# A state space layer inside a decoder step: the recurrence over chunks in two halves of four groups

## The chip, the cores and the metric

The kernel runs on one core of one Trainium2 chip. The core has five engines with queues of their own: TensorE (PE; its weight loads are shown as PEld), VectorE (DVE), ScalarE (ACT), GpSimd (POOL) and SyncE (SP). Each works through its own instructions strictly in the order of the program; semaphores make an instruction wait for those of other engines. The metric is the device time of one execution, in microseconds; lower is better. Before the change it is 1601.29 us, the median of three runs (1599.1 to 1602.14).

## The reference, cut to what matters

The program is one layer of a decoder on a prompt of 1024 tokens and on 8 single sample tokens. One input projection feeds two branches, stick-breaking attention and a state space layer; both are gated, projected, merged and normalised. The change touches the state space layer: 64 groups of 16 channels, each with a complex state of 64 numbers that decays and turns from token to token.

```python
bu_re = jnp.einsum("gpc,bsgc->bsgp", bb_re, ug)
bu_im = jnp.einsum("gpc,bsgc->bsgp", bb_im, ug)
...
_, _, xr, xi = lax.associative_scan(_complex_affine_combine,
                                    (a_re_t, a_im_t, bu_re, bu_im), axis=1)
y = (jnp.einsum("gcp,bsgp->bsgc", c_re.astype(f), xr)
     - jnp.einsum("gcp,bsgp->bsgc", c_im.astype(f), xi)).reshape(bsz, s, D_SSM)
y = y + d_skip.astype(f) * uf
g = jax.nn.gelu(y)
```

## The kernel before, in words

**Stages.** The program first modulates the activations, then runs the attention of the prompt beside the input projection (to about 740 us), then the state space layer (about 743 to 1115 us), then the gated linear unit, the output projections, the merge and the normalisation. In all stages a stream of projection matmuls (line 144, tiles named pj) fills PE between the other steps: `Stream.weave` takes a list of steps and runs a share of the stream ahead of each, so the order on PE is written out by hand. A step has a cost and may have a due time, in the stream's own clock of 146 ns for a matmul; the stream runs on until the clock has reached the due time or its work is used up. The order on the other engines is chosen at build time by a scheduler with a model of costs; `high_priority(HURRY)` lets instructions go ahead of those traced up to 400 places earlier.

**The state space layer.** It goes by slabs f = 0 to 7 of 128 channels, that is 8 groups, or 4 pairs of groups. The prompt is cut into 128 chunks of 8 tokens. Within a chunk everything is a product; from chunk to chunk runs the recurrence. A slab has these steps (`SSM.steps`):

- `outputs(f - 1, b)` for b = 0, 1: the output products of the slab before, four groups each, two matmuls a group. One reads the slab's inputs (line 1052), the other the states xs at the chunks' starts (line 1053). Then a GELU on ACT and DVE (lines 1085 to 1090, tiles gh and gq) and a store. The due time is "xs", set 17000 ns of stream clock after the last input product.
- `inputs(f, e, b)`: the input products (line 1002). e is the group's place in its pair (partitions 0 to 63 or 64 to 127 of the state), b says which two of the four pairs. Each step is two matmuls, evacuated by ACT into sr and si, the real and imaginary part (lines 1004 and 1005), 128 chunk columns and 8 sample columns for every pair. The order is (e, b) = (0, 0), (0, 1), (1, 0), (1, 1).
- after (1, 1) `recur(f)`: the sample columns are copied aside by POOL (lines 1018, 1019); DVE turns sr and si by the phase tables ec and es (lines 1024 to 1029, six operations on 128x512), scans each pair's real and imaginary row with the decay r8 (line 1033, eight scans of 128 columns), and turns back into xs (lines 1038 to 1042, four operations on 128x512 and four on 64x512). POOL clears the first column of xs (line 1035) and copies the last states aside (line 1043).
- `tables(f + 1)`, `grouped(f + 1)` and `matrices(f + 1, b)`: loads and small products for the next slab (lines 926, 941, 947 and 956 among them).

**What runs between.** `SampleAttention` scores the sample tokens against the paged cache: POOL issues gathers into tile s_t (line 810), ACT copies two query columns (lines 823, 824), DVE multiplies and adds (line 833, s_sc), later the values (line 828, s_t). `tick` spreads its 122 pieces of work over the steps, two ticks to a step. So that the pieces keep pace with the layer, each first reads one column of `k.last`, a tile that the steps set: u when a slab's inputs are taken, sr after an input product with e = 1, gin in `matrices`, gh in the GELU. The first instruction of a gather (line 808, POOL), of a query copy (line 823, ACT) and of a value (line 818, DVE) is this read.

The projection's results are evacuated by ACT (line 1525 and 1527 for gates, line 975 for the layer's inputs) out of three PSUM tiles, and the weights' low parts are formed by POOL (line 109).

The tiles sr, si and xs have one buffer each, gh and gq two, and PSUM tile "a", which all products of the layer use, five.

Of the kernel before, what the change touches and what calls it, by code (L numbers as in the profile page):

```python
# [23 lines left out]
NCH = 128  # L24
# [125 lines left out]
class Stream:  # L150
# [63 lines left out]
    def weave(self, steps, until=0.0):  # L214

        n = len(steps)
        for i, (cost, ready, fn) in enumerate(steps):
            self.run(max(0.0, self.left - until) / (n - i + 1))
            want = ready() if ready else 0.0
            while self.clock < want and self.left > until + 1:  # L220
                if self.one() is False:
                    break
            fn()
            self.clock += cost
        self.drain(until)
# [248 lines left out]
def ssm_products(k, sp, io, f, b, after):  # L474
# [60 lines left out]
    for part_ in (phasors, inputs, outputs):  # L535
        part_()
        yield
# [3 lines left out]
class Attention:  # L541
# [189 lines left out]
    def steps(self, pairs):  # L731

        units = [(p, h, ms) for p in pairs for h in range(2) for ms in ((3, 0), (2, 1))]
        out = {p: [] for p in pairs}
        for u, (p, h, ms) in enumerate(units):
            s = self.score_steps(units[u + 1]) if u + 1 < len(units) else []
            t = [(860, (lambda key=(p, h, m): self.ready_at[key]) if j == ORDER[m][0] else None,
                  lambda t=(p, h, m, j): self.turn_step(t)) for m in ms for j in ORDER[m]]
            if not s:
                t += [(430, None, lambda: self.turn_step(None))] * LAG  # L740
            seq = []
            for n in (2, 2, 1, 1):
                seq += s[:n] + t[:1]
                s, t = s[n:], t[1:]
            out[p] += seq + t
        return self.score_steps(units[0]), out
# [154 lines left out]
class SSM:  # L901
# [91 lines left out]
    def inputs(self, f, e, b):  # L993
        k, nc, v = self.k, self.k.nc, self.v[f]
        if (e, b) == (0, 0):
            v["s"] = [self.t([128, 4, NCH + NS], n) for n in ("sr", "si")]
        sr, si = v["s"]
        half = slice(64 * e, 64 * e + 64)
        sp_ = self.ps.tile([128, 2, NCH + NS], F32, tag="a", name="sps")
        for i in range(2):  # L1000
            g = 2 * (2 * b + i) + e
            nc.tensor.matmul(sp_[:, i], v["gin"][:, g], v["ug"][:, g], start=True, stop=True)
        with k.tc.high_priority(HURRY):
            nc.scalar.copy(sr[half, 2 * b:2 * b + 2], sp_[0:64])
            nc.scalar.copy(si[half, 2 * b:2 * b + 2], sp_[64:128])
        if e == 1:
            k.last = sr[:, 2 * b, 0:1]
        if (e, b) == (1, 1):
            with k.tc.high_priority(HURRY):
                self.recur(f)  # L1010

    def recur(self, f):

        v = self.v[f]
        DVE, POOL = self.k.nc.vector, self.k.nc.gpsimd
        pr = slice(4 * f, 4 * f + 4)
        sr, si = v["s"]
        POOL.tensor_copy(self.ss[0][:, pr], sr[:, :, NCH:])
        POOL.tensor_copy(self.ss[1][:, pr], si[:, :, NCH:])
        ec, es = v["ec"], v["es"]  # L1020
        Z = [128, 4, NCH]
        t1, t2 = (self.t(Z, n, 2) for n in ("gh", "gq"))
        xr, xi = sr[:, :, 0:NCH], si[:, :, 0:NCH]
        DVE.tensor_tensor(t1, xi, es, ALU.mult)
        DVE.tensor_tensor(t2, xr, es, ALU.mult)
        DVE.tensor_tensor(xr, xr, ec, ALU.mult)
        DVE.tensor_tensor(xi, xi, ec, ALU.mult)
        DVE.tensor_tensor(xr, xr, t1, ALU.add)
        DVE.tensor_tensor(xi, xi, t2, ALU.subtract)
        for q in range(4):  # L1030
            r8 = v["r8"][:, q, 0:1].broadcast_to((128, NCH))
            for x in (xr, xi):
                DVE.tensor_tensor_scan(x[:, q], r8, x[:, q], 0.0, ALU.mult, ALU.add)  # L1033
        v["xs"] = xs = self.t([128, 4, 2, NCH + 1], "xs")
        POOL.memset(xs[:, :, :, 0:1], 0.0)
        for r in range(2):
            rows = slice(64 * r, 64 * r + 64)
            DVE.tensor_tensor(t1, xr, es if r else ec, ALU.mult)
            DVE.tensor_tensor(t2, xi, ec if r else es, ALU.mult)
            for e in range(2):  # L1040
                half = slice(64 * e, 64 * e + 64)
                DVE.tensor_tensor(xs[rows, :, e, 1:], t1[half], t2[half], ALU.add if r else ALU.subtract)
        POOL.tensor_copy(self.xf[:, 8 * f:8 * f + 8], xs[:, :, :, NCH].rearrange("p q e -> p (q e)"))
        self.mark("xs", 17000.0)

    def outputs(self, f, b):
        k, nc, v = self.k, self.k.nc, self.v[f]
# [16 lines left out]
    def steps(self, f):  # L1064

        R = lambda n: (lambda: self.at.get(n, 0.0))
        k = self.k
        two = lambda cost, n, fn, f: [(cost, R(n) if b == 0 and n else None, lambda b=b: fn(f, b)) for b in range(2)]
        out = []
        if f > 0:  # L1070
            out += two(1750, "xs", self.outputs, f - 1)
        if f < KT:
            out += [(454, R("ug") if (e, b) == (0, 0) else None, lambda e=e, b=b: self.inputs(f, e, b))
                    for e in range(2) for b in range(2)]
        if f + 1 < KT:
            out += [(0, None, lambda: self.tables(f + 1)), (0, lambda: k.taken.get(f + 1, 0.0), lambda: self.grouped(f + 1))]
            out += two(1300, "tab", self.matrices, f + 1)
        return out
# [14 lines left out]
    def finish_steps(self, last):  # L1093

        k, nc, io, out = self.k, self.k.nc, self.io, self.out
        PE, ACT, DVE, SP = nc.tensor, nc.scalar, nc.vector, nc.sync
        Z = [128, NPAIR, NS]
        v = {}

        def state():  # L1100
            h0 = [self.t(Z, n) for n in ("sr", "si")]
            SP.dma_start(h0[0], io["h0_re"])
            SP.dma_start(h0[1], io["h0_im"])
            v["cb"] = [self.t([128, NPAIR, 2, GC], n, 2) for n in ("gst", "tt")]
            for c, src in zip(v["cb"], ("c_re", "c_im")):
                nc.gpsimd.memset(c, 0.0)
                for e in range(2):
                    half = slice(64 * e, 64 * e + 64)
                    SP.dma_start(c[half, :, e], io[src][half])
            v["mask"] = self.t([128, 16, 32], "es", 2)  # L1110
            SP.dma_start(v["mask"], io["mask"])
            v["pick"] = self.t([128, NS], "r8", 2)
            SP.dma_start(v["pick"], io["pick"])
            v["dc"] = self.t([128, KT], "r8", 2)
            SP.dma_start(v["dc"], io["d_col"])
            ar, ai = (self.a1[:, :, n:n + 1].broadcast_to(Z) for n in range(2))
            t = self.t(Z, "hst")
            for dst, (a, x, op1), (b, y, op2) in (
                    (self.ss[0], (ar, h0[0], ALU.add), (ai, h0[1], ALU.subtract)),
                    (self.ss[1], (ar, h0[1], ALU.add), (ai, h0[0], ALU.add))):  # L1120
                DVE.tensor_tensor(t, a, x, ALU.mult)
                DVE.tensor_tensor(dst, dst, t, op1)
                DVE.tensor_tensor(t, b, y, ALU.mult)
                DVE.tensor_tensor(dst, dst, t, op2)
            v["ni"] = self.t(Z, "yy", 2)
            DVE.tensor_scalar(v["ni"], self.ss[1], -1.0, None, op0=ALU.mult)
# [598 lines left out]
```

## Time and profile before

The profiled execution took 1602.6 us; its span, from the first to the last instruction, is 1600.9 us.

| | whole span | 743 to 1115 us |
|---|---|---|
| length | 1600.9 us | 372 us |
| PE busy | 1490.8 us | 340.7 us |
| DVE busy | 1200.7 us | 300.6 us |
| ACT busy | 752.6 us | 149.1 us |
| POOL busy | 931.9 us | 215.7 us |
| granted PE clock | 0.969 | 0.96 |

How to read the lines that follow. A line of a timeline gives the start, the duration, the engine, the line of the code, the operation, the tiles written and read with their shape, how many such instructions follow one another, and, in brackets, how long the engine stood idle before it and what ended the wait. A line of waits gives the engine and line that waited, what for, the total, how often, and the longest. A line of a source view gives the shortest, median and longest duration in ns and the first and the last start. The granted clock is the share of full speed that the throttle gave PE. Busy times of PE include pipelining, so a busy PE is not PE at its peak.

### The profile page before, as it was taken

The numbers are of one execution on the slowest core, as the hardware profiler recorded it, in microseconds if no ns is written. First come the engines' busy times: TensorE is split into PE (matmuls) and PEld (weight loads), VectorE is DVE, ScalarE is ACT, GpSimd is POOL, SyncE is SP. The second block draws the span as 40 slices with busy tenths as digits, with TensorE's granted clock in tenths as the row PEclk, the third lists the DMA queues.
The fourth block names the chain that finished last, engine by engine and source line by source line (L and its number), as shares of the span: only waits on it lengthen the run. The fifth ranks groups of instructions, "written<-read, shape, count | busy, mean of one in ns | idle before, by whom it ended". The sixth has DMA issues, their size and how long they took to land.

```text
span 1600.9 us, 25589 instructions
## 1 busy us (share of the span) xinstructions
PE 1490.8 (93%) x9321; PEld 1412.0 (88%) x9321; DVE 1200.7 (75%) x1533; ACT 752.6 (47%) x1488; POOL 931.9 (58%) x800
## 2 busy tenths in 40 slices
PE   8889999999999999999999998899989968999997
PEld 4689999999999999999899998898789967999885
DVE  5558888888888889751899877788479986844566
ACT  3557777777777767654444443332442212311200
POOL 1738787878786878766565555554168761122064
PEclk9899999999999999999999998899989979999999
DMA  9333433433343434348779987867455678963322
GB/s 353 114 86 88 106 101 99 101 98 97 99 102 92 113 88 118 94 121 285 243 252 291 290 273 236 273 217 203 134 184 186 212 254 285 364 207 132 119 80 92
DMA packets 176731, 275.47 MB, mean 172 GB/s; under 512 B 46395, under 2 KB 119867, under 8 KB 176477
## 3 DMA queue, kind: packets, MB, share of 16 engines
q1 hardware_dynamic: 150555, 180.40, 36.5%
q0 software_dynamic: 23456, 84.95, 16.6%
q10 hardware_dynamic: 2594, 8.49, 2.0%
q8 instruction: 73, 1.20, 0.3%
q14 instruction: 53, 0.43, 0.1%
HBM read 196.77 MB, written 66.24 MB: 164 GB/s over the span
## 4 chain that ended last, share of the span: by engine, by line
PE 47%; DVE 24%; issue 8%; DMA 8%; POOL 6%; ACT 2%; SPq 1%; DVEq 0%; POOLq 0%; ACTq 0%
PE pj L144 29%; PE f L1402 6%; PE o L703 3%; PE z L657 3%; DVE s_sc L833 3%; DVE ke L668 3%; PE tp L686 3%; DMA l_t<-in_cache_v,l_idx 2%; DVE vs L639 2%; DVE be L669 2%; POOL s_t L810 2%; DVE l_t L889 1%; POOL wlo L109 1%; DVE sr L1033 1%; DVE s_t L828 1%
## 5 line engine op out<-in xcount | busy, mean ns | idle before, releaser
L144 PE MATMUL pj<-ahi,whi 128*128 128x344 f32 x2112 | 690.6, 330 | 20.1 <-ACT ahi L237 11.3
L144 PE MATMUL pj<-alo,whi 128*128 128x344 f32 x2112 | 684.2, 327 | 10.7 <-DVE alo L238 6.9
L144 PE MATMUL pj<-ahi,wlo 128*128 128x344 f32 x2112 | 478.5, 328 | 6.2 <-POOL wlo L109 6.2
L144 PEld LDWEIGHTS pj<-ahi,whi 128*128 128x128 f32 x2112 | 404.5, 192 | 27.6 <-ACT ahi L237 12.1
L144 PEld LDWEIGHTS pj<-alo,whi 128*128 128x128 f32 x2112 | 405.2, 192 | 15.2 <-DVE alo L238 8.3
L144 PEld LDWEIGHTS pj<-ahi,wlo 128*128 128x128 f32 x2112 | 362.9, 192 | 8.0 <-POOL wlo L109 6.8
L668 DVE TENSOR_TENSOR_SCAN ke<-ke,eye 128x896 f32<-128x896 f32 (+7 forms) x128 | 218.8, 1710 | 93.8 <-ACT ke L658 93.7
L109 POOL TENSOR_TENSOR wlo<-w,whi 128x1024 fp32r<-128x1024 f32 x53 | 133.6, 2520 | 204.8 <-PE pj L144 108.9
L658 ACT ACTIVATE ke<-z,nhb 128x448 f32<-128x448 f32 (+2 forms) x192 | 111.8, 582 | 81.3 <-PE z L657 79.3
L108 ACT CAST whi<-w 128x1024 fp32r<-128x1024 f32 x90 | 94.7, 1052 | 115.7 <-PE pj L144 73.1
L669 DVE TENSOR_TENSOR be<-be,ke 128x896 f32<-128x896 f32 (+7 forms) x128 | 125.0, 977 | 13.0 <-DVE ke L668 0.5
L833 DVE SCALAR_TENSOR_TENSOR s_sc<-s_t,s_q,s_sc 128x512 f32<-128x512 f32 x126 | 114.0, 905 | 27.3 <-DMA s_t<-in_cache_k,s_idx 15.8
L659 ACT ACTIVATE be<-z,hb 128x448 f32<-128x448 f32 (+2 forms) x192 | 110.6, 576 | 0.0
L686 PE MATMUL tp<-ident,be 128*128 128x128 f32 x576 | 88.9, 272 | 0.0
L810 POOL DMA_INDIRECT s_t<-in_cache_k,s_idx x64 | 69.6, 1088 | 30.1 <-issue 15.4
L495 POOL TENSOR_TENSOR pr<-tab 128x256 f32<-128x256 f32 x32 | 26.0, 813 | 90.6 <-DMA tab<-d_tab 80.3
L496 POOL TENSOR_TENSOR pt<-tab 128x256 f32<-128x256 f32 x64 | 75.9, 1187 | 3.1
L109 DVE TENSOR_TENSOR wlo<-w,whi 128x1024 fp32r<-128x1024 f32 x37 | 62.0, 1676 | 15.9 <-ACT whi L108 15.9
L689 ACT CAST wthi<-tp 128x512 fp32r<-128x512 f32 x96 | 56.7, 590 | 32.3 <-PE tp L686 29.9
L657 PE MATMUL z<-kl,qs 128*128 128x448 f32 (+2 forms) x192 | 65.9, 343 | 4.0 <-DMA kl<-kl 4.0
L690 DVE TENSOR_TENSOR wtlo<-tp,wthi 128x512 fp32r<-128x512 f32 x96 | 65.3, 680 | 5.6 <-ACT wthi L689 5.4
L657 PE MATMUL z<-kh,qs 128*128 128x448 f32 (+2 forms) x192 | 66.3, 345 | 0.9
(314 smaller groups left out, 2760.8 us busy)
## 6 DMA issues: line engine op xcount, KB each, us to landing
w<-in_w_in SPq DMA_DIRECT2D x38, 512.0 KB
w<-in_w_in POOLq DMA_DIRECT2D x26, 512.0 KB, 6.3
wc<-in_w_cond SPq DMA_DIRECT2D x24, 512.0 KB
d_a<-ox SPq DMA_DIRECT2D x128, 64.0 KB
gst<-d_gg SPq DMA_DIRECT2D x8, 576.0 KB
x<-in_xr SPq DMA_DIRECT2D x9, 512.0 KB
xt<-in_xt SPq DMA_DIRECT2D x8, 516.0 KB
d_sg<-gate SPq DMA_DIRECT2D x8, 516.0 KB
```

Of the source, the lines that this page charges most:

```text
L108: nc.scalar.copy(whi, w32)
L109: self.eng.tensor_tensor(wlo, w32, whi.bitcast(F32), ALU.subtract)
L144: PE.matmul(ps[c], w[:, blk(t)], x[:, cs(c)], start=(t == 0 and i == 0), stop=(t == KT - 1 and i == 2))
L657: nc.tensor.matmul(z[:, 0:wide], st["q", h][:, blk(i)], x[:, s:s + wide], start=j == 0, stop=j == 1)
L658: nc.scalar.activation(ke[:, s:s + cw], z[:, 0:cw], AF.Sigmoid, bias=k.nhb[:, hd:hd + 1], scale=-0.125)
L659: nc.scalar.activation(be[:, s:s + cw], z[:, 0:cw], AF.Sigmoid, bias=k.hb[:, hd:hd + 1], scale=0.125)
L668: nc.vector.tensor_tensor_scan(rev, rev, self.eye[:, NP - n:][:, ::-1], 0.0, ALU.mult, ALU.add)
L669: nc.vector.tensor_tensor(be, be, ke[:, 1:n + 1], ALU.mult)
L686: PE.transpose(tp[:, 2 * order[a] + e], w[e][:, blk(2 * j + a)], k.ident)
L810: nc.gpsimd.indirect_dma_start(out=tile[:, j].rearrange("p d s -> p (d s)"), out_offset=None, in_=self.io["cache_" + what], in_offset=bass ...
L833: DVE.scalar_tensor_tensor(sc, t, q[:, d - d0:d - d0 + 1], sc, op0=ALU.mult, op1=ALU.add)
L1402: PE.matmul(pp[c], a[:, token(i)], w[:, blk(c, 512)], start=(t == 0 and a is ah and w is wh), stop=(t == KT - 1 and a is al))
```

## The change

The recurrence of a slab is cut into two halves of two pairs (four groups) each. `recur(f, b)` does for the pairs 2b and 2b + 1 what `recur(f)` did for all four; it is called after each input product with e = 1, and the order of the input products becomes (e, b) = (0, 0), (1, 0), (0, 1), (1, 1), so that half 0's two products come first. The tile xs is taken at the first input product, the temporaries gh and gq are taken once for both halves, the due time "xs" is set by the second half as before. Tiles, buffers and PE's instructions are otherwise the same.

```diff
     def inputs(self, f, e, b):
         k, nc, v = self.k, self.k.nc, self.v[f]
         if (e, b) == (0, 0):
+            v["xs"] = self.t([128, 4, 2, NCH + 1], "xs")
             v["s"] = [self.t([128, 4, NCH + NS], n) for n in ("sr", "si")]
...
         if e == 1:
             k.last = sr[:, 2 * b, 0:1]
-        if (e, b) == (1, 1):
             with k.tc.high_priority(HURRY):
-                self.recur(f)
-
-    def recur(self, f):
+                self.recur(f, b)
+
+    def recur(self, f, b):
 
         v = self.v[f]
         DVE, POOL = self.k.nc.vector, self.k.nc.gpsimd
-        pr = slice(4 * f, 4 * f + 4)
-        sr, si = v["s"]
+        two = slice(2 * b, 2 * b + 2)
+        pr = slice(4 * f + 2 * b, 4 * f + 2 * b + 2)
+        sr, si = (x[:, two] for x in v["s"])
         POOL.tensor_copy(self.ss[0][:, pr], sr[:, :, NCH:])
         POOL.tensor_copy(self.ss[1][:, pr], si[:, :, NCH:])
-        ec, es = v["ec"], v["es"]
-        Z = [128, 4, NCH]
-        t1, t2 = (self.t(Z, n, 2) for n in ("gh", "gq"))
+        ec, es = v["ec"][:, two], v["es"][:, two]
+        if b == 0:
+            v["t"] = [self.t([128, 4, NCH], n, 2) for n in ("gh", "gq")]
+        t1, t2 = (t[:, two] for t in v["t"])
...
-        for q in range(4):
-            r8 = v["r8"][:, q, 0:1].broadcast_to((128, NCH))
+        for q in range(2):
+            r8 = v["r8"][:, 2 * b + q, 0:1].broadcast_to((128, NCH))
             for x in (xr, xi):
                 DVE.tensor_tensor_scan(x[:, q], r8, x[:, q], 0.0, ALU.mult, ALU.add)
-        v["xs"] = xs = self.t([128, 4, 2, NCH + 1], "xs")
-        POOL.memset(xs[:, :, :, 0:1], 0.0)
+        if b == 0:
+            POOL.memset(v["xs"][:, :, :, 0:1], 0.0)
+        xs = v["xs"][:, two]
...
-        POOL.tensor_copy(self.xf[:, 8 * f:8 * f + 8], xs[:, :, :, NCH].rearrange("p q e -> p (q e)"))
-        self.mark("xs", 17000.0)
+        POOL.tensor_copy(self.xf[:, 8 * f + 4 * b:8 * f + 4 * b + 4], xs[:, :, :, NCH].rearrange("p q e -> p (q e)"))
+        if b == 1:
+            self.mark("xs", 17000.0)
...
             out += [(454, R("ug") if (e, b) == (0, 0) else None, lambda e=e, b=b: self.inputs(f, e, b))
-                    for e in range(2) for b in range(2)]
+                    for b in range(2) for e in range(2)]
```

## The prediction, made before the changed kernel was run

> **What bounds the kernel now.** I read the page first, then busy time by stretch, then who TensorE waits for, then the order of instructions around those waits. The changed lines run in one stretch only, from the first input product (743 us) to the last output product (about 1115 us).
>
> ```profile
> span 1600.9 us, 25589 instructions
> ...
> 743.00:1115.00 372.00, 340.73 (x2201) 331.13 (x2200) 300.57 (x490) 149.09 (x385) 215.70 (x227) 0.96 0.82 262
> 790.00:835.00 45.00, 42.49 (x286) 41.12 (x285) 40.89 (x48) 17.14 (x51) 27.94 (x29) 1.00 0.82 266
> 835.00:880.00 45.00, 43.48 (x292) 42.18 (x292) 42.60 (x58) 21.31 (x64) 27.92 (x32) 1.00 0.92 289
> ```
>
> The columns are the stretch, its length, the busy time of PE, PEld, DVE, ACT and POOL with their instructions, the granted clock, the DMA share and GB/s. PE has 341 of the 372 us filled; it is the bound, and it stands for some 31 us. DVE has 301 us, but 40.9 and 42.6 of 45 in the second and third slab. The waits of PE in this stretch, and each one in the order of time:
>
> ```profile
> PE yp L1053 <- DVE xs L1042: 25.4, 9, 4.4
> PE pj L144 <- ACT gate L1525: 4.6, 1, 4.6
> PE pj L144 <- ACT zgate L1527: 1.2, 1, 1.2
> 776.71 0.49 PE L1053 MATMUL yp<-xs,gst 128*128 128x128 f32 x2 [3.94 <-DVE xs L1042]
> 868.05 0.49 PE L1053 MATMUL yp<-xs,gst 128*128 128x128 f32 x2 [1.51 <-DVE xs L1042]
> 913.70 0.49 PE L1053 MATMUL yp<-xs,gst 128*128 128x128 f32 x2 [2.52 <-DVE xs L1042]
> 962.67 0.79 PE L1053 MATMUL yp<-xs,gst 128*128 128x128 f32 x2 [4.21 <-DVE xs L1042]
> 1018.53 0.80 PE L1053 MATMUL yp<-xs,gst 128*128 128x128 f32 x2 [4.43 <-DVE xs L1042]
> 1021.66 0.80 PE L1053 MATMUL yp<-xs,gst 128*128 128x128 f32 x2 [1.91 <-DVE xs L1042]
> 1113.33 0.80 PE L1053 MATMUL yp<-xs,gst 128*128 128x128 f32 x2 [3.94 <-DVE xs L1042]
> ```
>
> In every slab PE arrives at the first half of the output products (b = 0) before the recurrence has written xs: 25.4 us in nine waits. These products also come out slow (0.63 to 0.80 us where 0.49 is usual), so I looked at the granted clock (after the instruction count) in the 8 us behind a wait:
>
> ```profile
> 868.00:876.00 8.00, 7.94 (x57) 1.00 0.72 275
> 776.00:784.00 8.00, 7.28 (x40) 0.79 0.91 304
> 913.00:921.00 8.00, 7.29 (x39) 0.79 0.58 208
> 962.00:970.00 8.00, 7.33 (x43) 0.79 0.54 195
> 1018.00:1026.00 8.00, 5.56 (x22) 0.50 0.97 359
> 1113.00:1121.00 8.00, 7.67 (x39) 0.60 0.28 98
> ```
>
> After the 1.51 us wait the clock stays at 1.00; after each wait of 2.5 us or more it falls. (1 - clock) x 8 us summed over the five low windows is 3 x 1.7 + 4.0 + 3.2 = 12.2 us. PE stood for 0.3 to 2.4 us inside them, so I take 10 us as a second price of the same waits. Together **35 us** hang on xs being late.
>
> [...]
>
> **The change part by part.** Why xs is late is seen in the fourth slab (f = 3):
>
> ```profile
> 881.83 0.62 PE L1002 MATMUL sps<-ug,gin 128*128 128x136 f32 x4
> 889.69 0.63 PE L1002 MATMUL sps<-ug,gin 128*128 128x136 f32 x4
> 889.13 8.57 DVE L833 SCALAR_TENSOR_TENSOR s_sc<-s_t,s_q,s_sc 128x512 f32<-128x512 f32 x8 [5.17 <-DMA s_t<-in_cache_k,s_idx]
> 897.62 0.69 DVE L1025 TENSOR_TENSOR gq<-sr,es 128x512 f32<-128x512 f32 x1
> 901.24 3.97 DVE L1033 TENSOR_TENSOR_SCAN sr<-r,sr 128x128 f32<-128x128 f32 x4
> 912.96 1.41 DVE L1042 TENSOR_TENSOR xs<-gh,gq 64x512 f32<-64x512 f32 x2
> ```
>
> The second input product is issued at 881.83, the fourth at 889.69. DVE stands 5.17 us for a gathered tile, scores eight columns of it, and only then begins the recurrence (897.62), which ends at 914.4.
>
> *Inputs reordered.* b outside e: the same four products in the same four steps. The first two now complete half 0, so it may begin two steps (7.9 us here) before the old one. PE gains or loses no instruction.
>
> *Half 0 ahead of half 1.* Output products b = 0 read pairs 0 and 1 only, and waits go by region: PE started at 913.70, when the first of the two xs writes of 912.96 was done (0.70 each) and the second was not. So b = 0 will wait for half 0 alone. Even if half 0 starts no sooner than the old recurrence and simply takes the first half of its time, it is early enough. Slab 3: the old one runs 897.6 to 914.4, its middle is 906, PE needs it at 913.7 - 2.5 = 911.2. The tightest is slab 5:
>
> ```profile
> 1000.03 0.68 DVE L1025 TENSOR_TENSOR gq<-sr,es 128x512 f32<-128x512 f32 x1
> 1017.79 3.81 DVE L1042 TENSOR_TENSOR xs<-gh,gq 64x512 f32<-64x512 f32 x2
> 873.44 0.38 PE L1052 MATMUL yp<-ug,tt 128*128 128x128 f32 x2
> ```
>
> It runs 1000.0 to 1021.6, middle 1010.8, needed at 1018.5 - 4.4 = 1014.1. The waits for b = 0 go: 25.4 us, with the 10 us of clock.
>
> *What is late next:* half 1 for b = 1, which PE reaches 5.4 us after b = 0 (868.05 to 873.44). In slab 3 that is 911.2 + 5.4 = 916.6; the whole recurrence, starting no sooner and 2.3 us longer (next point), ends at 916.7, just in time. In slab 5 it is needed at 1019.5 and ends at 1023.9, 4.4 us late. Bounds: nothing, if half 0 starts its two steps sooner, and 4.4 us in all eight slabs, 35 us. Most slabs are nearer to slab 3 (their waits above are shorter than slab 5's), so I take 3 us.
>
> *DVE, twice as many instructions.* 14 tensor operations per slab on 512 columns become 28 on 256; the eight scans stay.
>
> ```profile
> L1025 DVE TENSOR_TENSOR gq<-sr,es x8: 683/685/693, 754.7 to 1094.2; 128x512 f32<-128x512 f32 x8
> L1122 DVE TENSOR_TENSOR ssr<-ssr,hst 128x256 f32<-128x256 f32 x1 | 0.4, 426 | 0.1
> L1018 POOL COPY ssr<-sr x8: 214/363/734, 755.1 to 1091.8; 128x32 f32<-128x32 f32 x8
> L1043 POOL COPY xf<-xs x8: 181/327/1503, 777.4 to 1114.1; 128x8 f32<-128x8 f32 x8
> ```
>
> 2 x 426 - 685 = 167 ns per pair, 14 pairs: 2.3 us per slab, 19 us in all. DVE is idle 372 - 301 = 71 us of the stretch, so it hides there; with that cover gone it is the second rival.
>
> *POOL* gets three more copies per slab (two of the first kind and one of the second, 2 x 0.36 + 0.33 = 1.05 us, 8 us in all) beside 156 idle us. But two of its copies now wait in the middle of the recurrence, and behind them on its queue stand the issue of the gathers and the low parts of the weights (L109).
>
> *The pacing tile k.last.* From the second step on the sample's loads and query copies read sr[:, 0] after half 0's scan; until now they read it from the third step on, before the scan. So ACT (s_q copies), POOL (tile marks) and later DVE (s_acc) get a wait on half 0. Behind the ACT copies stand the evacuations of the third and fourth input product and of the projection's PSUM (L1525).
>
> ```profile
> ACT s_q L823 <- DVE sr L1033: 38.0, 5, 11.5
> 953.95 0.47 ACT L823 COPY s_q<-sr 128x1 f32<-128x1 f32 x4 [11.46 <-DVE sr L1033]
> 992.74 1.15 ACT L840 ACTIVATE s_ke<-s_sc,s_bias 128x1024 f32<-128x1024 f32 x1 [11.74 <-DMA w<-in_w_in]
> 995.21 0.66 PE L144 MATMUL pj<-ahi,whi 128*128 128x344 f32 x1 [4.63 <-ACT gate L1525]
> ```
>
> ACT already waits so once in five slabs. An ACT wait of 11.46 us cost PE nothing; one of 11.74 us cost it 4.63 us. The new waits are two per slab, each on half the work. Bounds: 0 (all below 11 us) and 4.6 us in each of eight slabs, 37 us. All five old ones together left PE at most its 1.2 us wait for zgate, so I stay near that end: 4 us.
>
> *After the stretch.* PE gets ahead of the sample's gathers, which DVE waits for as it is:
>
> ```profile
> DVE s_sc L833 <- DMA s_t<-in_cache_k,s_idx: 15.8, 4, 6.1
> DVE s_t L828 <- DMA s_t<-in_cache_v,s_idx: 9.6, 3, 6.1
> ```
>
> If these seven waits grow by what PE gains, part of it comes back at the end of the stretch, where layer outputs stand behind the scoring on DVE. Bounds 0 and the whole 25.4 + 10; I take 6 us, a quarter of the 25 us that DVE waits for gathers now.
>
> **Sum**: 25.4 + 10 - 3 - 4 - 6 = 22 us off. The profiled execution took 1602.6 us (span 1600.9 and 1.7 around it), 1.3 us above the median of 1601.29. 1602.6 - 22 = 1580.6, by the median **1579 us**.
>
> **Rivals.** (1) *Forecast*, 12 to 36 us off: 1565 to 1589.
>
> (2) *DVE or the gathers hold PE.* For: 42.6 of 45 us in slab 2, a DMA share of 0.82 to 0.92, and the order on DVE, which is fixed and puts scores that wait for a gather ahead of the recurrence (889.13). Against: DVE's 301 + 19 = 320 us is less than PE's 341. Then half 1 is late in all eight slabs by 2.2 us, half way between slab 3 and slab 5: 18 us of the 35 are lost, and 6 to 10 more behind the stretch. That leaves 7 to 11 off, about 1592 us.
>
> [...]
>
> (3) *ACT is held* (the slower side). The s_q copies stand ahead of the evacuations of products three and four, and half 0 is late because DVE stands at a gather. It decides from an ACT wait of about 11.5 us. The price is 4.63 us and 1.7 us of clock (as above) per slab, 51 us in eight, less the 35: 16 slower, 1617; from six slabs on (38 us) the kernel is slower. Against: half 0 has only 6 x 0.43 us on DVE ahead of its scans, and the five ACT waits of now cost next to nothing.
>
> (4) *No effect within 3 us*: the order on DVE leaves half 0 behind the same scores and new waits eat the rest, 1598 to 1604. That waits go by whole tiles, so that half 0 would wait for all four evacuations, is excluded by 913.70.
>
> **How the numbers follow.** Forecast 0.55, rival 2 0.18, rival 4 0.10, rival 3 0.17. Faster by over 0.2% (3 us, about what a measurement of this kernel can tell): 0.55 + 0.18 = 0.73; within 0.10; slower 0.17. The range runs from the forecast's best end, 1565, over rivals 2 and 4 to 1605, which leaves rival 3 and a little more out.
>
> **What would show it.** Right: PE's wait for xs falls from 25.4 to under 6 us; the first DVE operation of half 0 comes before the fourth input product; the clock over the stretch rises from 0.96 to about 0.99; DVE busy there is up some 19 us; the stretch is 20 to 30 us shorter. Wrong: PE waits at L144 for L1525 in several slabs (3); b = 1 products wait for xs while b = 0 do not, or DVE never idles (2); the stretch is shorter but waits for gathers or for L1224 and L1225 behind it have grown as much (the last term).

## The result and the profile after

The changed kernel takes 1589.78 us (median of 6 runs, 1585.67 to 1591.82), the kernel before, timed beside it, 1599.62 us (1595.86 to 1602.14). The ratio is 0.9932, interval 0.9914 to 0.9949: faster by some 10 us, where 22 were forecast. The profiled spans differ by 10.8 us (1600.9 and 1590.1). First, where the span lost it. These are the source views of the line of the input products and of the line of the output products' first matmuls, of before and of after (shortest, median and longest duration in ns, first and last start):

```profile
L1002 PE MATMUL sps<-ug,gin x128: 277/279/280, 743.8 to 1090.9; 128*128 128x136 f32 x128
L1052 PE MATMUL yp<-ug,tt x128: 270/275/422, 772.4 to 1120.2; 128*128 128x128 f32 x128
```

```profile
L1003 PE MATMUL sps<-ug,gin x128: 277/279/280, 742.8 to 1074.4; 128*128 128x136 f32 x128
L1056 PE MATMUL yp<-ug,tt x128: 270/275/421, 771.4 to 1104.1; 128*128 128x128 f32 x128
```

The stretch from the first start of the one to the last start of the other went from 376.4 to 361.3 us, 15.1 shorter. Ahead of it 1.0 us is gained, which the change can't reach; what follows it went from 480.7 to 486.0, 5.3 longer. So -1.0 - 15.1 + 5.3 = -10.8.

What PE waits for in this stretch and just behind it, in the changed kernel (total, times, longest):

```profile
PE pj L144 <- ACT gate L1529: 12.7, 6, 5.1
PE pj L144 <- ACT zgate L1531: 5.7, 1, 5.7
PE ycr L1158 <- DVE yy L1130: 4.4, 1, 4.4
...
PE pj L144 <- ACT u L975: 1.5, 1, 1.5
PE pj L144 <- ACT us_s L977: 1.4, 1, 1.4
PE yp L1057 <- DVE xs L1045: 1.0, 1, 1.0
```

The nine waits for xs, 25.4 us, have become one of 1.0. But PE's waits for ACT at the projection, 4.6 + 1.2 = 5.8 us before, are 12.7 + 5.7 + 1.5 + 1.4 = 21.3. So 24.4 us went and 15.5 came; and ycr, the first product behind the stretch, waits 4.4 us where it waited 1.4. The clock, first the one low window of before that the prediction did not count, then those of after (the clock stands behind the last instruction count):

```profile
995.00:1003.00 8.00, 7.79 (x36) 7.79 (x37) 7.86 (x15) 4.16 (x8) 4.38 (x4) 0.69 0.54 153
```

```profile
820.00:828.00 8.00, 7.07 (x33) 7.07 (x34) 5.23 (x6) 5.37 (x15) 7.67 (x6) 0.59 0.89 336
942.00:950.00 8.00, 7.29 (x37) 7.29 (x38) 7.86 (x19) 2.81 (x7) 3.67 (x5) 0.79 0.64 210
1094.00:1102.00 8.00, 7.16 (x36) 7.16 (x37) 5.85 (x20) 2.18 (x5) 0.86 (x2) 0.65 0.63 208
799.00:807.00 8.00, 7.91 (x40) 7.91 (x41) 7.86 (x12) 3.23 (x8) 5.45 (x7) 0.79 0.92 326
```

By the prediction's rule, (1 - clock) x 8 us, the kernel before lost 12.2 us in its five windows and 2.5 in this sixth; the changed one loses 3.3 + 1.7 + 2.8 + 1.7 = 9.5 in four. That is 5.2 us recovered, not 10: behind the new waits the clock fell (to 0.59 to 0.79) as it did behind the old ones (0.50 to 0.79). Waits 24.4 - 15.5 = 8.9 and clock 5.2 make 14.1 of the 15.1 us. Some low stretches are longer than these windows; added up in steps of 2 us over the whole stretch, the loss by the same rule is 17.1 us before and 10.2 after, 6.9 recovered.

The new waits one by one, from PE's timeline of the changed kernel:

```profile
799.09 0.52 PE L144 MATMUL pj<-ahi,whi 128*128 128x344 f32 x1 [1.76 <-ACT gate L1529]
820.93 0.65 PE L144 MATMUL pj<-ahi,whi 128*128 128x344 f32 x1 [5.69 <-ACT zgate L1531]
930.58 0.43 PE L144 MATMUL pj<-ahi,whi 128*128 128x344 f32 x1 [1.49 <-ACT u L975]
942.71 0.65 PE L144 MATMUL pj<-ahi,whi 128*128 128x344 f32 x1 [3.84 <-ACT gate L1529]
...
1094.84 0.66 PE L144 MATMUL pj<-ahi,whi 128*128 128x344 f32 x1 [5.08 <-ACT gate L1529]
```

And what ACT itself stood for ahead of them, from its timeline:

```profile
820.43 0.80 ACT L1531 COPY zgate<-pj 128x344 f32<-128x344 f32 x2 [7.14 <-DMA d_sg<-gate]
...
940.76 0.28 ACT L823 COPY s_q<-sr 128x1 f32<-128x1 f32 x2 [5.48 <-DVE sr L1035]
...
986.36 0.19 ACT L823 COPY s_q<-sr 128x1 f32<-128x1 f32 x1 [9.79 <-DVE sr L1035]
...
1094.33 0.81 ACT L1529 ACTIVATE gate<-pj 128x344 f32<-128x344 f32 x2 [15.31 <-DMA d_ma<-gate]
```

Three causes, as the traces show them. The largest two PE waits (5.69 + 5.08 = 10.8 us) are ACT's wait for a buffer of the gate tile until its store has landed; there are two buffers, and a gate of kind g takes both, one for gate and one for zgate. Some 6.5 us lie behind query copies that wait for the scan (942.71, 799.09 and 0.90 us at 987.98; at 799.09 the profile names no releaser, but the copy starts at 796.78, when the first scan of 796.27 is done). Another 3.5 lie behind steps of ACT that wait for other work of DVE: two GELU steps (930.58, and 1.38 us at 1029.72) and the sigmoid of the scores (0.59 us at 992.61).

### The profile page after: what moved, and what is told of

Read it like the earlier page. It is cut to its first block, busy times and chain, and to the rows that moved or that the text cites. A ratio compares the mean times of both kernels' runs of the same rounds, so it can differ in the third digit from the quotient of the medians.

```text
span 1590.1 us, 25729 instructions
## 1 busy us (share of the span) xinstructions
PE 1486.1 (93%) x9321; PEld 1405.8 (88%) x9321; DVE 1209.4 (76%) x1645; ACT 752.4 (47%) x1488; POOL 936.3 (59%) x824
## 4 chain that ended last, share of the span: by engine, by line
PE 51%; DVE 22%; DMA 8%; issue 6%; ACT 4%; POOL 3%; SPq 0%; DVEq 0%; ACTq 0%; POOLq 0%
PE pj L144 33%; PE f L1406 6%; PE o L703 4%; PE z L657 3%; DVE ke L668 3%; PE tp L686 3%; DMA l_t<-in_cache_v,l_idx 3%; DVE s_sc L833 3%; DVE vs L639 2%; DVE be L669 2%; DMA s_t<-in_cache_k,s_idx 2%; DVE s_t L828 1%; DVE wlo L109 1%; DVE l_t L889 1%; DVE l_acc L890 1%
## 5 line engine op out<-in xcount | busy, mean ns | idle before, releaser
L144 PE MATMUL pj<-ahi,whi 128*128 128x344 f32 x2112 | 693.3, 331 | 35.8 <-ACT gate L1529 12.7
L144 PEld LDWEIGHTS pj<-ahi,whi 128*128 128x128 f32 x2112 | 405.8, 192 | 45.3 <-ACT gate L1529 14.3
L144 PEld LDWEIGHTS pj<-alo,whi 128*128 128x128 f32 x2112 | 406.1, 192 | 15.8 <-DVE alo L238 8.3
L668 DVE TENSOR_TENSOR_SCAN ke<-ke,eye 128x896 f32<-128x896 f32 (+7 forms) x128 | 223.6, 1747 | 93.2 <-ACT ke L658 93.0
L669 DVE TENSOR_TENSOR be<-be,ke 128x896 f32<-128x896 f32 (+7 forms) x128 | 118.0, 922 | 13.0 <-DVE ke L668 0.5
L833 DVE SCALAR_TENSOR_TENSOR s_sc<-s_t,s_q,s_sc 128x512 f32<-128x512 f32 x126 | 112.3, 891 | 19.3 <-DMA s_t<-in_cache_k,s_idx 12.2
L496 POOL TENSOR_TENSOR pt<-tab 128x256 f32<-128x256 f32 x64 | 72.7, 1136 | 3.1
```

Of the source, the lines that this page charges most:

```text
L144: PE.matmul(ps[c], w[:, blk(t)], x[:, cs(c)], start=(t == 0 and i == 0), stop=(t == KT - 1 and i == 2))
L496: POOL.tensor_tensor(t1, c, d, ALU.mult)
L668: nc.vector.tensor_tensor_scan(rev, rev, self.eye[:, NP - n:][:, ::-1], 0.0, ALU.mult, ALU.add)
L669: nc.vector.tensor_tensor(be, be, ke[:, 1:n + 1], ALU.mult)
L833: DVE.scalar_tensor_tensor(sc, t, q[:, d - d0:d - d0 + 1], sc, op0=ALU.mult, op1=ALU.add)
```

## The experiments

All changes are against the kernel before or the changed one, as said; ratios are to the kernel before. The expectations call A the theory that the pacing copies eat the gain, B that DVE is late, C that the store of the gate tile holds ACT.

### Is it the early start?

Two runs take the change apart. One has the two halves but calls them one behind the other after the fourth product, in the old order of products:

```diff
             k.last = sr[:, 2 * b, 0:1]
+        if (e, b) == (1, 1):
             with k.tc.high_priority(HURRY):
-                self.recur(f, b)
+                self.recur(f, 0)
+                self.recur(f, 1)
...
-                    for b in range(2) for e in range(2)]
+                    for e in range(2) for b in range(2)]
```

> Two halves, but both called after the fourth input product in the old order: nothing begins sooner, only the output products b = 0 can go on half 0. By the prediction's count b = 0 waits vanish and b = 1 is late by up to 4.4 us in a slab; 19 us less of xs waits. Theory A: the query copies wait for half 1's scan alone, once per slab as before, so few new ACT waits: ratio 0.990 to 0.994, as good as the change. Theory B: 19 us more of DVE with nothing sooner: ratio 0.996 to 1.002.

The other is the kernel before with the new order of products alone, the last line of that diff the other way round.

> The kernel before with the new order of the input products and the whole recurrence after the fourth. All theories: no change, ratio 1.000 within 0.002, xs waits 22 to 28 us. If it gains 0.3% or more, part of the change's effect is the order alone.

Halves called late: 1.0042 (1.0026 to 1.0057), slower than either theory allowed. Order alone: 0.9987 (0.9968 to 1.0007), no difference. PE's waits, of the first and of the second:

```profile
PE pj L144 <- ACT gate L1531: 16.6, 2, 9.0
PE yp L1059 <- DVE xs L1047: 10.1, 4, 6.0
PE pj L144 <- ACT zgate L1533: 9.1, 1, 9.1
```

```profile
PE yp L1053 <- DVE xs L1042: 25.3, 8, 9.0
```

The split alone brings the price (25.7 us of waits for gates, 4.9 for ycr) and takes away only 15 us of xs; the new order alone does nothing. Only the two together pay, and the early start of half 0 needs both. The traces bear that out on the whole: against the start of the fourth input product, half 0 begins between 4.5 us earlier and 5.1 later in the changed kernel (1.2 later in the middle of the eight slabs), and between 2.2 us earlier and 14.9 later with the halves called late (4.5 in the middle).

### The pacing copies (theory A)

Here k.last is a sample column of sr that no scan writes, so a query copy no longer waits for the scan. The same edit was made in the changed kernel and in the kernel before, where the copies ahead of the recurrence are no longer tied to it either:

```diff
-            k.last = sr[:, 2 * b, 0:1]
+            k.last = sr[:, 2 * b, NCH:NCH + 1]
```

> The change, with the pacing read of sr moved from column 0, which the recurrence rewrites, to sample column 128, which it does not: no query copy waits for a scan any more. Theory A (the gain was eaten by ACT, held at query copies behind half 0's and half 1's scans): PE's waits for ACT at the projection fall from 21 us to 8 or less, ACT's wait for the scan goes from 65 us to 0, 8 to 12 us faster than the change, ratio to the kernel before about 0.986. Theory B (DVE cannot keep up; ACT would wait for it anyway, at the GELU): ACT's waits move to the GELU, 0 to 3 us, ratio about 0.992. Theory C (gate stores behind waiting loads on SP's queue): the two waits of 5 us or more stay, 3 to 5 us faster, ratio about 0.990.

> The kernel before, with the same free pacing column. Theory A: before, ACT's waits for the scan cost PE at most 1.2 us, so nothing is to be had: ratio 1.000 within 0.002, xs waits still 20 us or more. If this column is worth as much here as on the change, the wait on the scan was no price of the change: ratio 0.995 or less.

The changed kernel stays where it was: 0.9936 (0.9909 to 0.9962). Its PE waits:

```profile
PE pj L144 <- ACT gate L1529: 11.1, 2, 5.8
PE pj L144 <- ACT zgate L1531: 4.9, 1, 4.9
PE yp L1057 <- DVE xs L1045: 4.2, 3, 2.5
```

ACT's waits for the scan are gone from the copies, and PE still waits 16 us for the gates: the two waits behind stores are there (4.93 us at 821.95, 5.84 at 1099.76), and 5.30 us at 994.54 are new, behind the sigmoid of the scores, for which ACT waits 9.1 us for DVE. The forecast of A falls. In the kernel before the edit costs time, 1.0055 (1.0039 to 1.0070):

```profile
PE yp L1053 <- DVE xs L1042: 33.9, 8, 9.5
```

So the edit has a price of its own, and what the copies cost in the changed kernel isn't settled by it. The price isn't a later recurrence: from the start of the fourth input product to the last write of xs the eight slabs take 207.2 us here and 206.7 before. Part of the rise from 25.4 to 33.9 is a wait that moved, since the 5.8 us that PE waited for gates before are 0.8 here. The rest stays open.

### The store of the gate tile (theory C)

Issued by POOL (kind g) and ACT (kinds m and a) instead of SP, in the changed kernel, in the one before, and in the changed one with the free pace added:

```diff
-        k.q["G"].dma_start(dst[f], t)
+        (nc.gpsimd if kind == "g" else nc.scalar).dma_start(dst[f], t)
```

> The change, with the stores of the gates issued by the engine that writes the gate last (POOL for the product, ACT for the others) instead of behind the loads on SP's queue. Theory C (PE now stands because ACT waits for one of the two gate tiles, whose store stands on SP's queue behind loads that wait for DVE): the waits of 5.7 and 5.1 us at the projection go, with some 3 us of clock, ratio about 0.985. Theory B (DVE too busy, whatever stands behind it): ACT's waits for the gate's store go but PE's waits come back as others, ratio 0.991 to 0.994.

> The kernel before with the same gate stores. Theory C: there PE lost 1.2 us to them, so next to nothing: ratio 0.998 to 1.001, xs waits still about 25 us. If it gains 0.5% or more, the store is a cost of its own and not one that the change uncovered.

> The change with both: gate stores off SP's queue, and the pacing column that no scan rewrites. Theory C with A as the second part: the query copies' waits (7 us of PE's) and the gate stores' (11 us) both go, ratio about 0.980, waits for ACT in the stretch under 6 us. Theory B: as the change, 0.992, with ACT's waits at the GELU.

Results: 1.0028 (1.0009 to 1.0048), 1.0079 (1.0055 to 1.0102) and 1.0020 (1.0003 to 1.0036). The move costs 0.8% even in the kernel before, so it can't test C cleanly. In the changed kernel PE's waits for zgate grew instead of going, from 5.7 to 17.0 us, the longest 14.9, and those for xs are 7.8 us. So a second try moved kinds m and a alone, to ACT, right behind their last sigmoid, and left kind g on SP:

```diff
-        k.q["G"].dma_start(dst[f], t)
+        (k.q["G"] if kind == "g" else nc.scalar).dma_start(dst[f], t)
```

> The changed kernel with the stores of the gates of kinds m and a issued by ScalarE, right behind the last sigmoid of each, instead of standing in the sync engine's queue behind the stores of yy; kind g is left as it is. Theory C: ScalarE's wait for the store of d_ma (15.3 us) goes, and with it the projection's waits for the gate in the second half of the stretch (5.1 us at 1094 us, part of the 3.8 at 942), so the time is 4 to 9 us below that of the changed kernel (ratio about 0.988 to 0.991). Theory B (VectorE is late in any case): another wait takes that place, and the ratio stays at 0.992 to 0.996. If the move itself costs (ScalarE issues 16 stores more), as moving all kinds did, it is 0.997 or above.

> The kernel before with the same move. Its projection waits 4.6 us for one gate in the stretch: by C the move brings it up to 4 us (ratio 0.997 to 1.000), otherwise none. Above 1.003 the move itself costs, and only the distance between this run and the run before it counts.

Changed kernel 0.9983 (0.9965 to 1.0001), kernel before 1.0053 (1.0034 to 1.0073): the move costs again, for a reason these runs don't settle. PE's waits in the changed kernel with it:

```profile
PE pj L144 <- ACT zgate L1531: 7.3, 2, 5.4
PE yp L1057 <- DVE xs L1045: 6.8, 2, 5.6
PE pj L144 <- ACT gate L1529: 6.0, 4, 3.6
```

The wait for the a gate at 1094 us is gone (12.7 falls to 6.0), but xs rises from 1.0 to 6.8. By the distance between the two runs, which the expectation names as the measure once the move costs, the split is worth 1608.83 - 1597.95 = 10.9 us with the move and 9.8 without: freeing the store gives back about 1 us, less than the runs can tell, where 4 to 9 were said. C is right about what held ACT at that place, and wrong that freeing it in this way gives the time back. The direct test, a third buffer for the gate tile, was not run.

### More room on DVE (theory B)

Half of the key scores are left out, in both kernels; the copies and gathers stay:

```diff
-            for d in range(d0, d0 + 2):
+            for d in range(d0, d0 + (1 if what == "k" else 2)):
```

> The kernel before with the same half of the key scores left out. It is the base for the run before this one. If VectorE's room alone governed the waits for xs, they would fall from 25.4 to under 15 us and the split would be worth less here than in the full kernel; if the length of the recurrence itself does (14 to 16 us from the last input product to its first output product), 20 to 25 us of them stay. Against the kernel before: 5 to 15 us faster by B, within 5 us if only that length counts.

> The changed kernel with every second step of the key scores' sum left out (the multiply-add of the second channel of each pair), about 63 of the 126 of 0.89 us in the stretch: VectorE has some 56 us more room there. The copies that pace them and the gathers stay. Theory B (ScalarE's new waits for the gate tile and the pacing copies go back to VectorE being late): the projection's waits for ScalarE in the key part of the stretch (before 960 us), 12.7 us with the 5.7 us of the zgate, fall below 5 us, the waits for xs stay under 2 us, and the time against the same cut made in the kernel before is 18 to 24 us lower, close to the forecast of 22. Theory C (the stores' own place in the queue holds the gate tile, whatever VectorE does): the waits stay at 10 us or more and the distance to the kernel before with the same cut stays at 8 to 12 us.

Whole recurrence: 1575.41 us, ratio 0.9841 (0.9820 to 0.9863). Halves: 1579.12 us, 0.9868 (0.9848 to 0.9888). The whole one is faster than either theory expected, and between the two no difference can be told. PE's waits, first of the whole recurrence, then of the halves:

```profile
PE yp L1053 <- DVE xs L1042: 11.0, 3, 6.7
PE pj L144 <- ACT zgate L1527: 5.9, 1, 5.9
```

```profile
PE pj L144 <- ACT gate L1529: 7.1, 2, 5.6
PE pj L144 <- ACT zgate L1531: 5.7, 1, 5.7
```

43 us of DVE's busy time are gone (1209.4 to 1166.1 us on the pages of the two kernels with halves). B's signs come out in part. In the kernel before, the xs waits fall below 15 us and the split is worth less, as B says. With halves, PE's waits for ACT ahead of 960 us fall from 12.7 to 5.7 us, close to B's 5 and far from C's 10; the wait left there is the one for the zgate (5.74 us at 815.39). But 7.1 us of waits for gates come in behind 960 us, behind GELU steps that wait for DVE, and neither theory's gain by the split (18 to 24 us, 8 to 12) is there. The runs show two other things. The xs waits of the whole recurrence fall from 25.4 to 11.0 us: from the fourth input product to the last xs the eight slabs take 172.0 us instead of 206.7, so more than half of these waits went with the scores on DVE. And the whole recurrence, once PE is early, meets the same zgate wait (5.9 us), with no split at all. The row behind it, ACT's copy, and the store on SP that it waits for, in the kernel before, in the changed one, and in this whole one with half the scores:

```profile
816.60 0.38 SPq L1530 DMA_DIRECT2D d_sg<-gate  x1
...
819.32 0.79 ACT L1527 COPY zgate<-pj 128x344 f32<-128x344 f32 x2 [3.78 <-DMA d_sg<-gate]
```

```profile
816.27 0.38 SPq L1534 DMA_DIRECT2D d_sg<-gate  x1
```

```profile
813.11 0.34 SPq L1530 DMA_DIRECT2D d_sg<-gate  x1
...
818.76 0.80 ACT L1527 COPY zgate<-pj 128x344 f32<-128x344 f32 x2 [9.49 <-DMA d_sg<-gate]
```

ACT goes on at 819.32, 820.43 and 818.76, though it was ready at 815.5, 813.3 and 809.3 (the start less the wait). It comes 2.3 and 6.2 us sooner, the store's issue only 0.3 and 3.5 us, and the end of the wait hardly moves. The store stands behind loads on SP's queue: POOL had finished the tile at 813.30, 809.38 and 807.36, so the issue came 3.3, 6.9 and 5.8 us after the tile was ready. That the loads ahead of it wait for buffers of the slab before was read from the trace, not tried.

### What the split is worth, and its toll

The pairs give one table. Saved is the fall of PE's xs waits by the split; worth is the difference of the medians, and beside it the difference of the two profiled executions, from which the waits are taken.

| base | xs waits, whole and halves | saved | worth, medians | worth, profiled executions |
|---|---|---|---|---|
| free pace | 33.9, 4.2 | 29.7 | 1609.68 - 1593.88 = 15.8 | 1604.24 - 1597.27 = 7.0 |
| as it is | 25.4, 1.0 | 24.4 | 1599.62 - 1589.78 = 9.8 | 1602.60 - 1591.82 = 10.8 |
| kinds m and a moved | 24.9, 6.8 | 18.1 | 1608.83 - 1597.95 = 10.9 | 1605.71 - 1599.09 = 6.6 |
| all stores moved | 22.1, 7.8 | 14.3 | 1612.95 - 1603.69 = 9.3 | 1607.44 - 1602.94 = 4.5 |
| half the key scores | 11.0, 0.6 | 10.4 | 1575.41 - 1579.12 = -3.7 | 1579.97 - 1576.75 = 3.2 |

In every pair of profiled executions less than half of what is saved at xs arrives; 7 to 23 us come back as other waits and lost clock. Against the medians the toll is some 14 us in three rows and 5 and 7 in the two with moved stores, but there waits of one execution stand against times of others, and each median is uncertain by some 3 us. That the split has a toll is shown; that it is a fixed sum is not.

The changed kernel run once more beside the others shows how steady this is:

> The change itself beside these, for the comparison on the same chip: ratio 0.993 within 0.003 by all theories.

It gives 0.9934 (0.9909 to 0.9959), with 18.0 us of waits for gates and 1.9 for xs. No version here that computes all of it beats the change.

## Why the prediction was right in sign and twice too large

**Right: the xs waits, 25.4 us.** They fell to 1.0. Halves called late take 15.3 of them away, the new order with them the rest. The sign given ("before the fourth input product") held in three slabs of eight (0, 2 and 3): in slab 2 half 0 began at 842.39 and the fourth product at 846.88, in slab 7 at 1079.12 and 1074.03. In five it began late and was still in time, as the prediction allowed. The prediction's rows show seven of the nine waits; the other two, 1.34 us at 823.37 and 1.66 at 1068.47, complete its sum, and the clock behind both is 1.00.

**Right: half 1 late, 3 us.** One wait of 1.0, in slab 6.

**Right that it hides, priced at twice its size: DVE, 19 us.** PE's waits for DVE in the stretch stayed small (1.0 us), and DVE's busy time over the whole span rose by 8.7 us only, from 1200.7 to

```profile
PE 1486.1 (93%) x9321; PEld 1405.8 (88%) x9321; DVE 1209.4 (76%) x1645; ACT 752.4 (47%) x1488; POOL 936.3 (59%) x824
```

The durations of two operations in a row overlap here (805.68 + 0.68 is 806.36, and the next starts at 806.28), so the price of one more is read from their starts, of before and of after:

```profile
805.68 0.68 DVE L1027 TENSOR_TENSOR si<-si,ec 128x512 f32<-128x512 f32 x1
806.28 0.68 DVE L1028 TENSOR_TENSOR sr<-sr,gh 128x512 f32<-128x512 f32 x1
```

```profile
1079.12 0.41 DVE L1027 TENSOR_TENSOR gq<-sr,es 128x256 f32<-128x256 f32 x1
1079.45 0.42 DVE L1026 TENSOR_TENSOR gh<-si,es 128x256 f32<-128x256 f32 x1
```

0.60 us against 2 x 0.33: 60 ns for one more operation, and 6.7 us for 112. The 167 ns of the prediction came from durations. POOL rose by 936.3 - 931.9 = 4.4 us, 8 were said.

**Wrong: the new waits for ACT, 4 us.** This is the step that failed: put at 4 us, it measured 15.5 by the rows of the result, and the 11.5 between them are half of the forecast. The prediction counted only the copies it had added (some 6.5 us here, and freeing them left the time where it was) and priced them by their length, with a threshold of about 11.5 us. But an ACT wait of 5.48 us cost PE 3.84 at 942, and one of 9.79 cost it 0.90 at 988. Rival 3 was right that PE would wait for ACT at the projection; its mechanism, the copies, covers less than half of these waits, and its price of 37 us of waits (51 with the clock) was too high. What it missed altogether is the gate tile, the next thing with a time of its own: its store was not in the list of what is late next. The row was there: PE's 1.2 us for zgate, behind an ACT wait of 3.78 us for that store, in a slab where PE was about to come earlier. The prediction put that 1.2 us down to the query copies.

**Wrong: the clock, 10 us.** 5.2 by the same rule (6.9 in steps of 2 us), since it was tied to the xs waits alone; the largest waits in their place are as long. The granted clock over the stretch went from 0.96 to 0.97, where 0.99 was said.

**Right in size, wrong in mechanism: 6 us given back behind the stretch.** 5.3 us, but the waits for gathers did not grow (15.8 and 9.6 before; now):

```profile
DVE s_sc L833 <- DMA s_t<-in_cache_k,s_idx: 12.2, 4, 5.9
DVE s_t L828 <- DMA s_t<-in_cache_v,s_idx: 9.3, 4, 3.7
```

The largest part is ycr, 1.4 to 4.4 us, and the clock behind it, of before and of after:

```profile
1132.00:1140.00 8.00, 6.14 (x13) 1.57 (x12) 1.39 (x2) 1.61 (x4) 0.00 (x0) 0.79 0.47 147
```

```profile
1118.00:1126.00 8.00, 7.12 (x8) 1.79 (x8) 0.69 (x1) 1.00 (x3) 0.00 (x0) 0.50 0.39 112
```

In steps of 2 us over the 40 us behind the stretch, 1.7 us of clock are lost before and 5.1 after. ycr waits 3.3 to 5.9 us in every run with halves and 1.4 in every run without, whatever else was edited, so the split brings it; its cause was not tried.

With the measured sizes the sum is 24.4 - 15.5 + 5.2 - 5.3 = 8.8 off. The spans show 10.8; 1.0 of it lies ahead of the stretch, and 1.0 is not in these terms.

The measured 1589.78 us lies just outside the forecast's own band (1565 to 1589). Rival 2 (1592 us) came nearest in time, but by luck: DVE did not make half 1 late.

## What to carry to other kernels

When a wait is removed from the bounding engine, list every producer that it will now meet earlier, with the time at which each is free by itself: a store that empties one of two buffers counts, and a wait of PE of 1.2 us on it was the sign here. Don't price a delay of the evacuating engine by its length alone: here 5.48 us of it cost PE 3.84, and 9.79 us cost 0.90. And ask what the removed wait is made of: here more than half of it went when half of the scores on VectorE were left out. That gave more than twice the split's gain and left the split nothing that could be told.

## What the runs showed of the hardware

**The clock fell after a shorter wait than the prediction took.** In the changed kernel a wait of 1.76 us (799.09) was followed by four microseconds at 0.57 of the clock; after 1.49 us (930.58) it stayed at 1.00:

```profile
799.00:803.00 4.00, 3.91 (x15) 3.91 (x16) 3.92 (x8) 3.23 (x8) 2.01 (x4) 0.57 0.85 297
...
930.00:938.00 8.00, 7.42 (x48) 7.42 (x49) 7.79 (x11) 4.31 (x9) 6.02 (x7) 1.00 0.79 221
```

The length alone doesn't decide it. In the stretch of the kernel before and of the changed one, none of PE's waits of 0.90 to 1.66 us was followed by a low clock (1.00 in the 4 us behind each of the eight), and every one of 2.52 us or more was (0.50 to 0.76 in the 4 us behind each of the nine). Between them lie the 1.76 us, followed by 0.57, and 1.91 us (1021.66) that fell in a clock already low. In the changed kernel with the free pace, the matmuls of line 144 read 0.32 us from 1.8 us behind a wait of 2.46 us (1017.59) on, as they did ahead of it; behind one of 2.71 us (899.85) they read 0.49.

**Operations of VectorE took 2.5 and 4.7 us longer beside operations of GpSimd.** The operation at 842.39, whose line has a median of 0.43 us, took 2.93 us while POOL formed a low part, and ended 0.3 us behind that:

```profile
842.39 2.93 DVE L1027 TENSOR_TENSOR gq<-sr,es 128x256 f32<-128x256 f32 x1
...
842.66 2.38 POOL L109 TENSOR_TENSOR wlo<-w,whi 128x1024 fp32r<-128x1024 f32 x1
```

In the kernel before, four scans took 6.06 us, over two such operations of POOL; the four behind them, at 814.78, took 1.36:

```profile
808.16 6.06 DVE L1033 TENSOR_TENSOR_SCAN sr<-r,sr 128x128 f32<-128x128 f32 x4
...
808.55 2.38 POOL L109 TENSOR_TENSOR wlo<-w,whi 128x1024 fp32r<-128x1024 f32 x1
810.90 2.40 POOL L1529 TENSOR_TENSOR gate<-gate,zgate 128x1032 f32<-128x1032 f32 x1
```

The 4.7 us that the scans lost are close to the 2.38 + 2.40 us of POOL, and the 2.5 us of the first operation to POOL's 2.38. Coming first did not spare the operation at 842.39, which stands 0.27 us ahead of POOL's. Why it took longer isn't shown. xs was 1.3 to 4.4 us late in the kernel before, so one such meeting, which cost 2.5 or 4.7 us here, is as large as what it was late by.
